# Splitting the weights of two products one product sooner and pinning activation splits behind them, in a retention and GLA layer

## The chip, the cores and the metric

The kernel runs on one core of a Trainium2 chip. The metric is device time in microseconds of one launch, the median of several runs. TensorE (PE) does the matmuls, VectorE (DVE) and ScalarE (ACT) the elementwise work, GpSimd (POOL) small vectors and adding DMAs, and SyncE (SP) issues most DMAs.

## The reference

One decoder layer over 512 rows and 16 meta rows of width 1024, in float32: an RMS norm, one wide input projection, a retention branch (4 heads, q and k of 256 with rope, v and gate of 512), a gated linear attention branch (4 heads), two branch projections, a merge by sigmoid gates, and an output projection with the residual and a last norm.

```python
u = rms_norm(h, norm_gain)
proj = u @ w_in
(rq, rk, rv, rg, gq, gk, gv, gg, glr, m_ret, m_gla) = jnp.split(proj, points, axis=-1)
rq = rope(rq.reshape(bsz, length, RET_HEADS, RET_QK_DIM), pos)
rk = rope(rk.reshape(bsz, length, RET_HEADS, RET_QK_DIM), pos) * (RET_QK_DIM ** -0.5)
o_ret = retention_chunked(rq, rk, rv)
o_ret = head_group_norm(o_ret, ...) * jax.nn.silu(rg)
...
merged = jax.nn.sigmoid(m_ret) * (o_ret @ w_branch_ret) + jax.nn.sigmoid(m_gla) * (o_gla @ w_branch_gla)
return h + merged @ w_out
```

## The kernel before

**Products in halves.** Every float32 operand of a matmul is split into a high half, which ACT casts (`nc.scalar.copy`), and a low half, which DVE takes as the difference; both are done by `split` (L163 in the profile). A product of two operands is then three matmuls: high by high, and the two mixed ones. For weights on the right side (`rows`) the order is high weight, low weight, high weight, so the second matmul of a product needs the low half.

**A quad.** Most projections go through `quad`, which computes a 1024 by 512 block with seven block products in place of eight (a Winograd form). In the order of the program these are products 1 (A11), 2 (A12), 6 (S2), 7 (S3), 5 (S1), 4 (A22) and 3 (S4). The name in brackets is the form of the activations, which is kept in both halves; the weights are split by `prepare`, which also keeps the pair of instructions in the list `low`. There are three buffers for each half, so a split has to wait until the product three before it is done. Three PSUM banks a, b and c take the sums: 1, 6, 5 and 3 go to b, 2 to a, 7 and 4 to c. Between the products `copy` brings a running sum out of PSUM (ACT), and `put` evacuates a finished quarter. Each product pins its first matmul behind the product before, so PE's order is the program's. Three flags move a split ahead of its product: `ahead` for product 2, `sooner` for product 6, `early` for another order of the products.

**Order of the work.** A planner orders the instructions of each engine: among those that it holds to be ready, the one that the program emitted first goes first. `after(a, b)` adds an edge that only tells the planner to put a behind b on their engine. `weave(dense, chain)` emits one step of the dense work (a product) and then one of the chain (smaller work).

**Heads 0 and 3.** For these two, the gate projection `ret_g` and the value projection `ret_v`, fourteen products, are the dense work. The chain is `ret_rope` (rope of k, split of k, rope of q, split of q: six steps) and then `ret_scores`. `every` adds, after each two steps of the rope, one step of the attention of the head before (`at`; none in head 0). In `ret_g` product 2's split is ahead. Its outputs carry the names rg_, those of `ret_v` rv_. The split q (qh, ql) is what the first score product needs, which stands on PE behind product 6 of `ret_v`. In `ret_v` the sums of raw weights stand at L364 and L365 (x3, x1), L381 (w11, which becomes product 6's) and L388 (w21, product 4's). Heads 1 and 2 order this work otherwise.

**Output projection.** Columns 0 to 255 are done plainly, columns 256 to 767 by a quad (names wo_), and the last 256 plainly again. The quad's chain is `merged_sums`, which makes the forms of the merged activations: the S2 and S3 forms, S1, then S4 from sums at L1519. For a quarter with `put(0, 0)` DVE adds (L1601, L1604) and ACT takes squares (fsq, L1556) for the last norm.

Of the kernel before, what the change touches and what calls it, by code (L numbers as in the profile page):

```python
# [25 lines left out]
ALU = mybir.AluOpType  # L26
# [14 lines left out]
C_RQ, C_RK, C_RV, C_RG = 0, 1024, 2048, 4096  # L41
# [7 lines left out]
A11, A12, A22, S1, S2, S3, S4 = range(7)  # L49
# [60 lines left out]
def hybrid_kernel(ctx: ExitStack, tc: tile.TileContext, I, out: bass.AP):  # L110
    nc = tc.nc
# [50 lines left out]
    def split(hi, lo, src):  # L162
        return nc.scalar.copy(hi, src), nc.vector.tensor_sub(lo, src, hi.bitcast(F32))  # L163
# [3 lines left out]
    def after(ins, prev):  # L167

        tc.add_manual_dep(ins.ins, prev.ins.name, mybir.DependencyInfo(
            mybir.DependencyClass.NoSync, mybir.DependencyReason.DATA), reason="order on an engine")  # L170
# [42 lines left out]
    def weave(dense, chain, skip=0):  # L213

        for n, _ in enumerate(dense):
            tick()
            if n >= skip:
                next(chain, None)
        for _ in chain:
            pass  # L220

    def every(gen, n, m=1, other=None):

        for i, _ in enumerate(gen):
            yield
            if i % m == m - 1:
                for _ in range(n - m):
                    if other is not None:
                        next(other, None)
                    yield  # L230

    def run(*gens):
        for g in gens:
            yield from g
# [29 lines left out]
    low = []  # L264

    def quad(cols, rows, name, evac, meta=None, adds=True, ahead=False, behind=None, src=None,
# [33 lines left out]
        if wide:  # L300
            a, b = [[ppt(f"{name}_{x}{t}")[:, :HT] for t in range(2)] for x in "cb"]
            c = a
# [13 lines left out]
        def product(i, form, w, ps, fresh, ready=None):  # L316
            hi, lo = ready or prepare(i, w)
            n = HT if wide and i not in (3, 5) else 256
            for t in range(2):
                col = slice(t * P, (t + 1) * P)  # L320
                for kk in range(4):
                    u = [row(f[form], kk)[:, col] if rows else row(f[form], kk)[:, :n] for f in forms]
                    v = [f[:, kk, :] if rows else f[:, kk, col] for f in (hi, lo)]
                    first = fresh and kk == 0 and (wide or t == 0)
                    for j, (x1, x2) in enumerate(((0, 0), (0, 1), (1, 0))):
                        l, r = (u[x1], v[x2]) if rows else (v[x1], u[x2])
                        m = nc.tensor.matmul(ps[t][:, :n] if wide else ps[t], l, r, start=first and j == 0,  # L327
                                             stop=kk == 3 and j == 2,
                                             skip_group_check=not fresh or not wide and t == 1)
                        if t == kk == j == 0:  # L330
                            pin(m)
            order[:] = [m]
# [13 lines left out]
        def put(n, th, x, y):  # L346
            evac(n, th, x if wide else x[2], y)
# [31 lines left out]
        else:  # L379
# [13 lines left out]
                late.append(lambda: meta(psm))  # L393
            yield
        product(5, S1, x1, b, False, ready)
        put(1, 1, b, x7)
        run_late()
        yield
        product(4, A22, w21, c, False)
        ready = prepare(3, w22) if early else None  # L400
        put(0, 1, c, y)
        yield
# [831 lines left out]
    def rope(t, c, name, prev=None):  # L1234

        def view(m):
            return m[:, :t.shape[2] * t.shape[3]].rearrange("p (h c) -> p h c", h=2)

        m = [view(rp.tile([P, 2 * HT], F32, tag="tmp", name=f"{name}_{i}", bufs=7)) for i in range(4)]
        x = nc.vector.tensor_mul(m[0], t[:, 0], c[0])  # L1240
        if prev is not None:
            after(x, prev)
            after(nc.vector.tensor_mul(m[1], t[:, 1], c[1]), prev)
        else:
            nc.vector.tensor_mul(m[1], t[:, 1], c[1])
        nc.vector.tensor_sub(m[0], m[0], m[1])
        yield
        nc.vector.tensor_mul(m[2], t[:, 1], c[0])
        nc.vector.tensor_mul(m[3], t[:, 0], c[1])
        nc.vector.tensor_add(m[2], m[2], m[3])  # L1250
        yield
        R[name] = m[0], m[2]
# [15 lines left out]
    def ret_rope(h):  # L1268
        q, k = R["raw", h]
        yield from rope(k, (cs[:, 0], cs[:, 1]), f"rpk{h}", None if h % 3 else low[1])  # L1270
        kh = rp.tile([P, 2, 2, HT], F32R, tag="kh", name=f"kh{h}")
        kl = rp.tile([P, 2, 2, HT], F32R, tag="kl", name=f"kl{h}")
        for i, m in enumerate(R[f"rpk{h}"]):
            split(kh[:, i], kl[:, i], m)
        for r in range(4):
            nc.gpsimd.tensor_copy(km[:, :, 32 * r:32 * r + NM].rearrange("p k (h m) -> p k h m", h=2),
                                  (kh if r < 3 else kl)[:, :, :, 256:HT].bitcast(F32))
        yield
        yield from rope(q, (cs[:, 0, :, :256], cs[:, 1, :, :256]), f"rpq{h}")
        qh = rp.tile([P, 2, T], F32R, tag="qh", name=f"qh{h}")  # L1280
        ql = rp.tile([P, 2, T], F32R, tag="ql", name=f"ql{h}")
        R["qk", h] = qh, ql, kh, kl
        for i, m in enumerate(R[f"rpq{h}"]):
            split(qh[:, i].rearrange("p (h c) -> p h c", h=2), ql[:, i].rearrange("p (h c) -> p h c", h=2), m)
        yield

    def ret_g(h):
        sg = rp.tile([P, 2304], F32, tag="sg", name=f"sg{h}")[:, :2048].rearrange("p (b c) -> p b c", b=NTB)
        R["sg", h] = sg
        yield from quad((C_RG + h * 512, C_RG + h * 512 + 256), True, f"rg{h}", rows_into(sg, AF.Silu),  # L1290
                        ahead=h % 3 == 0, behind=R.get(("pow", h - 1)))

    def ret_v(h):
        vh = rp.tile([P, NTB, 512], F32R, tag="vh", name=f"vh{h}")
        vl = rp.tile([P, 2176], F32R, tag="vl", name=f"vl{h}")[:, :2048].rearrange("p (b c) -> p b c", b=NTB)
        R["v", h] = vh, vl

        def meta(psm):
            ps = meta_rows(psm, f"rvm{h}")
            vm = rp.tile([P, 512], F32R, tag="vm", name=f"vm{h}")  # L1300
            nc.scalar.copy(vm, ps)
            nc.vector.tensor_sub(vm[64:96], ps[64:96], vm[64:96].bitcast(F32))
            R["vm", h] = vm

        def evac(n, th, x, y):
            if y is not None:
                s = tmp2(f"vs{h}{n}{th}")
                total(s, x, y)
                x = s
            d = slice(2 * th, 2 * th + 2), slice(n * 256, (n + 1) * 256)  # L1310
            hi, lo = vh[:, d[0], d[1]], vl[:, d[0], d[1]]
            if n == 0:
                split(hi, lo, x)
            else:
                nc.scalar.mul(hi, x, -1.0)
                nc.vector.scalar_tensor_tensor(lo, x, -1.0, hi.bitcast(F32), op0=ALU.mult, op1=ALU.subtract)

        yield from quad((C_RV + h * 512, C_RV + h * 512 + 256), True, f"rv{h}", evac, meta, False)

    def ret_scores(h):  # L1320
        qh, ql, kh, kl = R["qk", h]
# [152 lines left out]
    for h in range(4):  # L1474
        if h == 0:
            drain(ret_qk(h))
        else:
            at = ret_attention(h - 1)
            weave(ret_qk(h), at if h < 3 else islice(at, NTB + 1))
        if h % 3:  # L1480
            g = gates_gla(h - 1)
            weave(run(islice(g, 2), turns(ret_branch(h - 1), g)), ret_rope(h), skip=2)
            weave(ret_g(h), ret_scores(h))
            drain(ret_v(h))
        else:
            weave(run(ret_g(h), ret_v(h)), run(every(ret_rope(h), 3, 2, at if h else None), ret_scores(h)))
    weave(gates_ret(), ret_attention(3))

    def rows4(t, o, w, c):
# [9 lines left out]
    def merged_sums():  # L1499

        a = [[sigr[2 * kh + j][:, :, th * 256:(th + 1) * 256] for j in range(2)] for th in range(2) for kh in range(2)]
        a00, a01, a10, a11 = a

        def parts_of(i, x):
            for j in range(2):
                split(mforms[0][i][:, 2 * j:2 * j + 2], mforms[1][i][:, 2 * j:2 * j + 2], x[j])

        for j in range(2):
            nc.vector.tensor_sub(a11[j], a11[j], a10[j])
            nc.vector.tensor_sub(a10[j], a00[j], a10[j])  # L1510
        for j in range(2):
            nc.vector.scalar_tensor_tensor(a00[j], a11[j], -1.0, a00[j], op0=ALU.mult, op1=ALU.subtract)
        parts_of(S2, a00)
        yield
        parts_of(S3, a10)
        yield
        parts_of(S1, a11)
        for j in range(2):
            nc.vector.scalar_tensor_tensor(a01[j], a00[j], -1.0, a01[j], op0=ALU.mult, op1=ALU.subtract)  # L1519
        yield  # L1520
        parts_of(S4, a01)
        yield


# [124 lines left out]
```

## Time and profile before

| | |
|---|---|
| median of 3 runs | 751.62 us (750.5 to 751.65) |
| the profiled execution | 750.33 us |
| its span, first to last instruction | 748.6 us |
| ACT busy | 450.3 us (60%) |
| HBM read, written | 104.44 MB, 11.53 MB |

A row of a timeline gives the start in us, the duration in us, engine, line, operation, names (written, then read), shapes and, in brackets, idle time of the engine before it and what ended it. A row ending in x2 stands for two instructions in one. In a row of the list of waits stand the waiting instruction, what it waited for, the total in us, how often, and the longest. A matmul's end is modelled, its start is recorded.

### The profile page before, as it was taken

To read this page: it belongs to the slowest core of one execution; us is meant where nothing else is said; L and a number is where in the kernel's file an instruction comes from. 1 tells how busy PE (TensorE), PEld (TensorE's weight loads), DVE (VectorE), ACT (ScalarE), POOL (GpSimd) and SP (SyncE) were. 2 spreads that over 40 slices of the span, in tenths; PEclk is the share of its full clock that TensorE was granted. 3 is DMA by queue.
4 is the path that set the end of the run, shared out by engine and by line. 5 is a ranking of instruction groups with operands and counts; after the bars stand their busy time and mean duration, and the time that the engine had idled before them with its cause. 6 is when DMAs were issued, how large, how long until landed. Compare 5 with 4: busy or idle time off the path is not lost.

```text
span 748.6 us, 14064 instructions
## 1 busy us (share of the span) xinstructions
PE 738.6 (99%) x5595; PEld 691.7 (92%) x5595; DVE 607.7 (81%) x873; ACT 450.3 (60%) x764; POOL 137.5 (18%) x172
## 2 busy tenths in 40 slices
PE   9999999999999999999999999999999999999996
PEld 6799899989999999999989999989999989988996
DVE  6699877679897799888957688967697989775995
ACT  7898584666975466546546555646555656532562
POOL 2111110101221122110520100540011210111142
PEclk9999999999999999999999999999999999999999
DMA  9873521821589972734783652796476356687503
GB/s 298 278 162 77 121 62 53 198 85 58 129 187 280 305 169 87 170 113 141 200 250 115 133 149 96 199 213 163 126 169 136 113 141 197 227 195 206 133 29 113
DMA packets 100138, 117.42 MB, mean 157 GB/s; under 512 B 5732, under 2 KB 90852, under 8 KB 99816
## 3 DMA queue, kind: packets, MB, share of 16 engines
q1 hardware_dynamic: 79896, 88.19, 37.1%
q0 software_dynamic: 19888, 27.79, 20.4%
q8 instruction: 44, 0.72, 0.4%
q10 hardware_dynamic: 288, 0.53, 0.2%
q14 instruction: 22, 0.18, 0.1%
HBM read 104.44 MB, written 11.53 MB: 155 GB/s over the span
## 4 chain that ended last, share of the span: by engine, by line
PE 89%; DVE 7%; issue 2%; ACT 1%; POOL 0%; POOLq 0%; DVEq 0%; ACTq 0%
PE rqk_b L327 6%; PE rv_b L327 6%; PE rg_b L327 5%; PE rqk_c L327 5%; PE br_p L201 4%; PE br_p L202 4%; PE br_p L198 4%; PE gg_b L327 3%; PE mg_b L327 3%; PE mr_b L327 3%; PE gv_p L652 3%; PE rv_c L327 3%; PE bg_b L327 2%; PE rg_c L327 2%; PE gk_p L437 2%
## 5 line engine op out<-in xcount | busy, mean ns | idle before, releaser
L202 PE MATMUL br_p<-oh,br_l 128*128 128x512 f32 x128 | 49.9, 390 | 0.0
L201 PE MATMUL br_p<-ol,br_h 128*128 128x512 f32 x128 | 49.9, 390 | 0.0
L198 PE MATMUL br_p<-oh,br_h 128*128 128x512 f32 x128 | 49.8, 389 | 0.0
L163 ACT CAST rv_h<-rv_w 128x1024 fp32r<-128x1024 f32 x24 | 25.3, 1053 | 25.3 <-DVE rv_w L381 10.4
L327 PE MATMUL rqk_b<-xh,rqk_h 128*128 128x264 f32 (+1 forms) x128 | 36.2, 283 | 0.0
L327 PE MATMUL rqk_b<-xh,rqk_l 128*128 128x264 f32 (+1 forms) x128 | 36.1, 282 | 0.0
L327 PE MATMUL rqk_b<-xl,rqk_h 128*128 128x264 f32 (+1 forms) x128 | 36.0, 281 | 0.0
L327 PE MATMUL rv_b<-rv_l,xh 128*128 128x256 f32 x128 | 35.5, 277 | 0.5 <-DVE rv_l L163 0.5
L163 DVE TENSOR_TENSOR rv_l<-rv_w,rv_h 128x1024 fp32r<-128x1024 f32 x24 | 29.3, 1221 | 8.1 <-ACT rv_h L163 8.1
L327 PE MATMUL rv_b<-rv_h,xh 128*128 128x256 f32 x128 | 35.8, 280 | 0.0
L327 PE MATMUL rv_b<-rv_h,xl 128*128 128x256 f32 x128 | 35.4, 277 | 0.0
L327 PE MATMUL rg_b<-rg_h,xh 128*128 128x256 f32 x128 | 35.4, 277 | 0.0
L327 PE MATMUL rg_b<-rg_h,xl 128*128 128x256 f32 x128 | 35.4, 276 | 0.0
L327 PE MATMUL rg_b<-rg_l,xh 128*128 128x256 f32 x128 | 35.4, 276 | 0.0
L163 DVE TENSOR_TENSOR rg_l<-rg_w,rg_h 128x1024 fp32r<-128x1024 f32 x20 | 24.4, 1220 | 8.1 <-ACT rg_h L163 8.1
L163 ACT CAST rg_h<-rg_w 128x1024 fp32r<-128x1024 f32 x20 | 21.0, 1052 | 15.6 <-PE br_p L201 5.9
L291 POOL DMA_DIRECT2D rqk_x<-in_w_in_dram x8 | 10.4, 1302 | 102.2 <-PE rv_b L327 64.2
L202 PEld LDWEIGHTS br_p<-oh,br_l 128*128 128x128 f32 x128 | 24.0, 188 | 5.0
L1380 ACT ACTIVATE on<-av,nm,g_r 128x512 f32<-128x512 f32 x16 | 12.5, 779 | 26.4 <-DVE nm L1378 26.4
L198 PEld LDWEIGHTS br_p<-oh,br_h 128*128 128x128 f32 x128 | 24.0, 188 | 4.6
L201 PEld LDWEIGHTS br_p<-ol,br_h 128*128 128x128 f32 x128 | 24.0, 188 | 4.5
L163 ACT CAST rqk_h<-rqk_w 128x1024 fp32r<-128x1024 f32 x20 | 21.0, 1052 | 11.8 <-PE rqk_c L327 2.9
(624 smaller groups left out, 3155.4 us busy)
## 6 DMA issues: line engine op xcount, KB each, us to landing
rv_w<-in_w_in_dram SPq DMA_DIRECT2D x16, 512.0 KB, 4.2
br_w<-in_w_branch_ret_dram SPq DMA_DIRECT2D x16, 512.0 KB, 3.4
rqk_w<-in_w_in_dram SPq DMA_DIRECT2D x12, 512.0 KB, 5.0
rg_w<-in_w_in_dram SPq DMA_DIRECT2D x12, 512.0 KB, 4.9
rqk_x<-in_w_in_dram SPq DMA_DIRECT2D x8, 512.0 KB, 4.6
rqk_x<-in_w_in_dram POOLq DMA_DIRECT2D x8, 512.0 KB, 7.9
rg_x<-in_w_in_dram SPq DMA_DIRECT2D x8, 512.0 KB, 3.6
rg_x<-in_w_in_dram POOLq DMA_DIRECT2D x8, 512.0 KB, 7.6
```

Of the source, the lines that this page charges most:

```text
L163: return nc.scalar.copy(hi, src), nc.vector.tensor_sub(lo, src, hi.bitcast(F32))
L198: m = nc.tensor.matmul(o, lh, rh, start=first, stop=False)
L201: nc.tensor.matmul(o, lh, rl, start=False, stop=False)
L202: m = nc.tensor.matmul(o, ll, rh, start=False, stop=last)
L291: x = nc.gpsimd.dma_start(t, block(0, 1), accum_op=ALU.add)
L327: m = nc.tensor.matmul(ps[t][:, :n] if wide else ps[t], l, r, start=first and j == 0, stop=kk == 3 and j == 2, skip_group_check=not fresh ...
L437: m = nc.tensor.matmul(pss[t][th], l[:, kk, c], r, start=first and j == 0, stop=kh == 1 and kk == 3 and j == 2, skip_group_check=not meta ...
L652: m = nc.tensor.matmul(pss[t], (al if j == 1 else ah)[t // 2, kh][:, k, c], (lo if j == 2 else hi)[:, kk, :], start=q == kk == j == 0, sto ...
L1380: nc.scalar.activation(on, ps, AF.Identity, scale=r, bias=nm)
```

## The change

In `ret_g` of heads 0 and 3 the weights of product 4 are split before product 5's sum is evacuated. In `ret_v` of these heads the weights of product 6 are split before product 2's result is evacuated. In these heads the first two multiplications of q's rope are pinned behind the low half split last, and the splits of q come one step later and are pinned behind the pair split last. `every` now covers the first five steps of the rope, so the attention of the head before is stepped twice beside it. In the output projection the splits of S1, the sums for S4 and the splits of S4 come one or two steps later, and each is pinned behind the weights split last.

```diff
         product(5, S1, x1, b, False, ready)
+        ready = prepare(4, w21) if ahead else None
         put(1, 1, b, x7)
...
-        product(4, A22, w21, c, False)
+        product(4, A22, w21, c, False, ready)
...
-        yield from rope(q, (cs[:, 0, :, :256], cs[:, 1, :, :256]), f"rpq{h}")
+        yield from rope(q, (cs[:, 0, :, :256], cs[:, 1, :, :256]), f"rpq{h}", None if h % 3 else low[1])
...
+        if h % 3 == 0:
+            yield
+        prev = () if h % 3 else list(low)
         for i, m in enumerate(R[f"rpq{h}"]):
-            split(qh[:, i].rearrange("p (h c) -> p h c", h=2), ql[:, i].rearrange("p (h c) -> p h c", h=2), m)
+            s = split(qh[:, i].rearrange("p (h c) -> p h c", h=2), ql[:, i].rearrange("p (h c) -> p h c", h=2), m)
+            for ins, p in zip(s, prev):
+                after(ins, p)
...
-        yield from quad((C_RV + h * 512, C_RV + h * 512 + 256), True, f"rv{h}", evac, meta, False)
+        yield from quad((C_RV + h * 512, C_RV + h * 512 + 256), True, f"rv{h}", evac, meta, False, sooner=h % 3 == 0)
...
-            weave(run(ret_g(h), ret_v(h)), run(every(ret_rope(h), 3, 2, at if h else None), ret_scores(h)))
+            rp_h = ret_rope(h)
+            weave(run(ret_g(h), ret_v(h)), run(every(islice(rp_h, 5), 3, 2, at if h else None), rp_h, ret_scores(h)))
...
-        def parts_of(i, x):
+        def parts_of(i, x, prev=()):
             for j in range(2):
-                split(mforms[0][i][:, 2 * j:2 * j + 2], mforms[1][i][:, 2 * j:2 * j + 2], x[j])
+                s = split(mforms[0][i][:, 2 * j:2 * j + 2], mforms[1][i][:, 2 * j:2 * j + 2], x[j])
+                for ins, p in zip(s, prev):
+                    after(ins, p)
...
-        parts_of(S1, a11)
+        yield
+        parts_of(S1, a11, list(low))
+        yield
         for j in range(2):
-            nc.vector.scalar_tensor_tensor(a01[j], a00[j], -1.0, a01[j], op0=ALU.mult, op1=ALU.subtract)
-        yield
-        parts_of(S4, a01)
+            after(nc.vector.scalar_tensor_tensor(a01[j], a00[j], -1.0, a01[j], op0=ALU.mult, op1=ALU.subtract), low[1])
+        yield
+        parts_of(S4, a01, list(low))
         yield
```

## Prediction

> **What bounds the kernel now.** I read the page first, for which engine sets the time; then the list of PE's waits, for where PE stands; then PE's timeline at those places, since a matmul's end is modelled and only starts can be trusted; last the timelines of DVE and ACT there, for what is late.
>
> ```profile
> span 748.6 us, 14064 instructions
> PE 738.6 (99%) x5595; PEld 691.7 (92%) x5595; DVE 607.7 (81%) x873; ACT 450.3 (60%) x764; POOL 137.5 (18%) x172
> ```
>
> PE is nearly always at work, so a change that leaves PE's instructions alone (this one adds and removes no matmul) can only win the time in which PE stands.
>
> ```profile
> PE rg_c L327 <- DVE rg_l L163: 0.6, 1, 0.6
> PE wo_c L327 <- DVE wo_l L163: 0.5, 1, 0.5
> PE rv_b L327 <- DVE rv_l L163: 0.5, 1, 0.5
> PE wo_b L327 <- ACT wo_x L343: 0.3, 1, 0.3
> ```
>
> Each of these waits occurs once in the whole run. The first and third lie in head 3 and the other two in the output projection, as the next view shows; head 0, which runs the same code as head 3, has none.
>
> ```profile
> 593.22 0.28 PE L327 MATMUL rg_c<-rg_h,xh 128*128 128x256 f32 x1
> 594.11 0.39 PE L327 MATMUL rg_c<-rg_l,xh 128*128 128x256 f32 x1 [0.62 <-DVE rg_l L163]
> 594.34 0.28 PE L327 MATMUL rg_c<-rg_h,xl 128*128 128x256 f32 x1
> ...
> 607.14 0.28 PE L327 MATMUL rv_b<-rv_h,xh 128*128 128x256 f32 x1
> 607.93 0.38 PE L327 MATMUL rv_b<-rv_l,xh 128*128 128x256 f32 x1 [0.51 <-DVE rv_l L163]
> ...
> 718.95 0.28 PE L327 MATMUL wo_c<-wo_h,msh 128*128 128x256 f32 x1
> 719.75 0.39 PE L327 MATMUL wo_c<-wo_l,msh 128*128 128x256 f32 x1 [0.52 <-DVE wo_l L163]
> ...
> 722.26 0.28 PE L327 MATMUL wo_c<-wo_l,msh 128*128 128x256 f32 x1
> 722.37 0.28 PE L327 MATMUL wo_c<-wo_h,msl 128*128 128x256 f32 x1
> 722.96 0.39 PE L327 MATMUL wo_b<-wo_h,mh 128*128 128x256 f32 x1 [0.31 <-ACT wo_x L343]
> 723.29 0.39 PE L327 MATMUL wo_b<-wo_l,mh 128*128 128x256 f32 x1
> 723.51 0.28 PE L327 MATMUL wo_b<-wo_h,ml 128*128 128x256 f32 x1
> ```
>
> The undisturbed pace is 0.11 us from start to start (722.26 to 722.37). Start to start minus the pace is what a wait costs, which is more than the list of waits says. Product 4 of ret_g in head 3: 0.89 - 0.11 = 0.78, and the next matmul comes 0.23 - 0.11 = 0.12 late as well: 0.90. I take the same 0.12 behind the next two waits too, as an estimate. Product 6 of ret_v: 0.79 - 0.11 + 0.12 = 0.80. Product 7 of the output projection: 0.80 - 0.11 + 0.12 = 0.81. Product 5 there: 0.59 - 0.11 = 0.48 for the first matmul, 0.33 - 0.11 = 0.22 for the second (the weight's low half), 0.22 - 0.11 = 0.11 for the third: 0.81. All four together are 3.3 us. That is the most that the four places can give.
>
> **Head 3.** In each of them the second matmul is late, the one that needs the low half of the split weights, which DVE makes.
>
> ```profile
> 587.91 1.05 ACT L163 CAST rg_h<-rg_w 128x1024 fp32r<-128x1024 f32 x1
> ...
> 588.13 1.22 DVE L163 TENSOR_TENSOR rg_l<-rg_x,rg_h 128x1024 fp32r<-128x1024 f32 x1
> 589.26 0.68 DVE L844 TENSOR_TENSOR sg<-rg_a,rg_x 128x512 f32<-128x512 f32 x1
> ...
> 592.84 1.22 DVE L163 TENSOR_TENSOR rg_l<-rg_w,rg_h 128x1024 fp32r<-128x1024 f32 x1
> ...
> 595.51 0.68 DVE L844 TENSOR_TENSOR sg<-rg_b,rg_x 128x512 f32<-128x512 f32 x1
> ```
>
> *Product 4 split a product sooner, q's rope behind it.* The high half was ready at 588.96 (587.91 + 1.05); the low half ran only at 592.84. Between lie evacuations and, emitted before product 4, q's first rope step. With the split emitted before both and q's two first multiplications pinned behind it, the low half can run from 589.26 and end by 590.5, against PE's 593.33. That holds even if an evacuation or two of 0.6 go first. So this wait goes: 0.90. What is late next is DVE itself. Product 3 adds into the same PSUM bank that the evacuation at 595.51 reads until 596.19, and PE, 0.90 earlier, would come at about 596.0 (product 4's first matmul at 593.22, and 24 at 0.11 to 0.12). So some 0.2 us of a new wait is likely there. It does not enter the sum, because the next point decides.
>
> ```profile
> 599.64 0.68 DVE L163 TENSOR_TENSOR ql<-rpq,qh 128x512 fp32r<-128x512 f32 x1
> 600.25 1.22 DVE L364 TENSOR_TENSOR rv_x<-rv_w,rv_w 128x1024 f32<-128x1024 f32 x1
> 601.38 0.68 DVE L163 TENSOR_TENSOR ql<-rpq,qh 128x512 fp32r<-128x512 f32 x1
> ...
> 604.25 1.22 DVE L381 TENSOR_TENSOR rv_w<-rv_w,rv_x 128x1024 f32<-128x1024 f32 x1
> 605.50 1.23 DVE L388 TENSOR_TENSOR rv_w<-rv_w,rv_w 128x1024 f32<-128x1024 f32 x1
> 606.65 1.23 DVE L163 TENSOR_TENSOR rv_l<-rv_w,rv_h 128x1024 fp32r<-128x1024 f32 x1
> ...
> 605.56 1.06 ACT L163 CAST rv_h<-rv_w 128x1024 fp32r<-128x1024 f32 x1 [0.30 <-DVE rv_w L381]
> ```
>
> *Product 6 split a product sooner, q's splits behind it.* Not one of DVE's rows here has idle time in front: DVE is the bound of this stretch, and what lies ahead of product 6's low half (606.65) decides. Emitting the split sooner gains nothing by itself. The sum L381 ends at 605.47, ACT casts from 605.56 to 606.62, and L388 just fills DVE's hole meanwhile. What gains is that q's two differences leave the queue ahead: 0.61 (599.64 to 600.25) and, at the same size, 0.6. The low half then starts at 605.45, and the second matmul, now at 607.93, comes at 606.73. PE, freed of the first wait, would ask for it at 607.14 - 0.90 + 0.11 = 606.35, or up to 0.2 later if the evacuation above holds it. DVE stays the later one, so head 3 gives 607.93 - 606.73 = **1.2 us**, not 1.70. Bounds: 1.70 if DVE has less ahead of it than I count, 0 if other work takes the place of q's. Below nothing only if q's halves now come too late for the scores; that is a rival below. Behind the pinned splits are queued product 7's split and the value evacuations. PE leaves product 6 for the first score product and needs q's halves there:
>
> ```profile
> 610.66 0.40 PE L198 MATMUL sc<-qh,kh 128*128 128x512 f32 x1
> ...
> 299.65 0.40 PE L198 MATMUL sc<-qh,kh 128*128 128x512 f32 x1
> ...
> 295.34 1.22 DVE L163 TENSOR_TENSOR rv_l<-rv_w,rv_h 128x1024 fp32r<-128x1024 f32 x1
> ```
>
> At 610.66 - 1.2 = 609.5 in head 3. The low half ends at about 606.6, one evacuation (0.6) and the two q differences (1.2) end at 608.4: 1.1 to spare. In head 0 the low half now ends at 296.56 and will end no later, q's at 298.4 at most, against 299.65. So **head 0: 0**; it has no wait to lose, and keeps 1.2 us of cover.
>
> No step that is moved issues a DMA, and SP's and POOL's queues keep their order. The attention of the head before is stepped twice instead of three times beside the rope, but by then it has one half-turn left to emit, so nothing moves. Heads 1 and 2 take no new edge.
>
> **Output projection.**
>
> ```profile
> 714.20 1.05 ACT L163 CAST wo_h<-wo_x 128x1024 fp32r<-128x1024 f32 x1
> ...
> 715.52 1.83 DVE L163 TENSOR_TENSOR ml<-sigr,mh 128x512 fp32r<-128x512 f32 x2
> 717.28 1.28 DVE L1519 SCALAR_TENSOR_TENSOR sigr<-sigr,sigr 128x512 f32<-128x512 f32 x2
> 718.48 1.21 DVE L163 TENSOR_TENSOR wo_l<-wo_x,wo_h 128x1024 fp32r<-128x1024 f32 x1
> 720.82 0.68 DVE L1604 TENSOR_TENSOR hs<-hs,wo_x 128x512 f32<-128x512 f32 x1
> ...
> 721.53 0.42 ACT L1556 ACTIVATE fsq<-hs 128x256 f32<-128x256 f32 x1 [1.37 <-DVE hs L1604]
> 722.35 0.56 ACT L343 COPY wo_x<-wo_b 128x512 f32<-128x512 f32 x1
> ```
>
> *S1 behind product 7's weights.* Product 7's high half is ready at 715.25, but S1's two differences and S4's two sums stand ahead on DVE until 718.48. Pinned behind, they free the place at 715.52: the low half ends at 716.7, PE asks at 719.06, and 0.81 goes with 2.3 us of cover. *The copy of product 6's sum.* PE's second wait is for the copy at 722.35, which on ACT follows the squares at 721.53, which wait for the sum L1604 at 720.82, late behind the same S1 and S4 work. The L1519 pair (1.2) and S4's split leave its way. At worst S1's two differences stay ahead of it: the low half ends at 716.7, then 1.2 for these, 0.6 for the sum before L1604 and 0.6 for itself, which makes 719.1. The squares take 0.82 (721.53 to 722.35) and end near 720.0, the copy (0.56) near 720.6; PE would ask at 722.48 - 0.81 = 721.7. The 0.81 goes too, with 1.1 of cover. *S4 behind products 5 and 4.* Its sums and splits are 4 x 0.6 = 2.4 us of DVE work, moved and not added. They are needed by product 3, two products of 24 matmuls (2.7 each) after product 5's start; DVE then has three weight differences (1.15 each, the step from 605.50 to 606.65) beside them, so it is through in time. **1.6 us**, bounds 0.8 (the copy stays late) and 1.6.
>
> **Sum.** 1.2 + 0 + 1.6 = 2.8 us. The work in between is paced by PE, so the gain is carried to the end. The profiled execution took 750.33 us (748.6 of span) and would be 747.5. The median shown is 751.62, with runs from 750.5 to 751.65, and 751.62 - 2.8 = 748.8 is the forecast.
>
> **Rivals.** *A: DVE keeps head 3.* If the low half of product 6 is queued straight behind L381, L388 no longer fills the hole in which ACT casts (1.15, from 605.50 to 606.65), and product 7's split and q's halves come that much later; head 3's 1.2 is lost there again. Against it: the planner filled that hole before. Time: 751.62 - 1.6 = 750.0. [...]
>
> *B: given back.* New waits of the size of those removed, at the evacuation of 595.51 and around S4, take 2.8 back: 751.6. For it: two of my covers are 1.1 us. Against it: the only place where I find PE ahead of what it needs is product 3 of ret_g, and there by 0.2.
>
> *C: slower, by q's halves.* The pin takes whatever pair was split last when q's splits are emitted. If that pair belonged to a later product (4), whose buffer comes free only as product 6 ends, PE would stand at the first score product for a cast (1.06), a difference (1.15) and q's two (1.2): 3.4 us in each of heads 0 and 3, so 751.62 - 2.8 + 6.8 = 755.6. It decides from a lateness of 2.8 + 1.5 = 4.3 over both heads. Against it: the product's step is emitted before q's in the same turn, so the pair is product 6's. *D: it does not do what it says*, since edges change only the planned order and the planner already orders so: true of head 0, contradicted by the rows for the rest; it is within B.
>
> **How the numbers follow.** Forecast 0.64, A 0.20, B 0.10, C 0.06. The low end is 747.5, the profiled execution's time less 2.8. The high end leaves out B and C (0.16): it is A with the copy still late, 0.8, less 0.3 of a new wait: 751.1. A measurement of this kernel can tell about 0.2%, 1.5 us, from no change. The forecast lies beyond that, A on the line: faster 0.64 x 0.97 + 0.2 x 0.45 = 0.71, slower 0.06, same 0.23.
>
> **What would show it.** Right: PE's list of waits without wo_c and wo_b, rg_c without its 0.6, rv_b at most 0.4; DVE's ql behind product 6's rv_l in heads 0 and 3; wo_l for product 7 straight behind product 6's; a span of 745.8. Wrong: a new PE wait at sc (C), at rg_b for ACT or DVE at product 3, or DVE idle before product 6's rv_l (A); or waits in heads 1 and 2, which I hold untouched.

## The result and the profile after

The changed kernel takes **748.37 us** (median of 18 runs, 747.8 to 750.52) against 750.97 us (18 runs, 749.88 to 752.43) for the kernel before on the same chip. The ratio is 0.9969, 95% interval 0.9961 to 0.9977: 750.97 x 0.0031 = 2.3 us faster, 1.7 to 2.9 (the two medians alone lie 2.6 apart). The forecast was 748.8, from 2.8 us.

The profiled execution of the kernel after took 750.22 us, hardly less than the 750.33 of before. Here is the head of its page, and then two rows of its list of PE's waits (the waiting instruction, what it waited for, total, how often, longest).

```profile
span 748.4 us, 14064 instructions
PE 739.1 (99%) x5595; PEld 692.2 (92%) x5595; DVE 608.5 (81%) x873; ACT 449.7 (60%) x764; POOL 135.7 (18%) x172
```

```profile
PE bg_b L327 <- DVE gs L1153: 0.9, 1, 0.9
...
PE rg_b L327 <- DVE sg L845: 0.2, 1, 0.2
```

The engines do the same work as before (DVE 608.5 against 607.7): it was moved, not removed. All four waits that the prediction listed (rg_c, rv_b, wo_c, wo_b) are gone from the list. Two are new: rg_b, 0.2, which the prediction expected at product 3 of ret_g, and bg_b, 0.9, at a place that the change does not touch. The next view, PE's timeline of the kernel after, shows this one.

```profile
228.89 0.38 PE L327 MATMUL bg_b<-gs,bg_h 128*128 128x256 f32 x1
230.15 0.39 PE L327 MATMUL bg_b<-gs,bg_h 128*128 128x256 f32 x1 [0.88 <-DVE gs L1153]
```

This is in the GLA branch, ahead of head 0: 1.26 us from one matmul to the next. With 0.8 us that PE was late ahead of it, this hides the gain in this execution's span, so the span alone says nothing of the change. What can be read is PE's order, which is the same in both kernels: 5595 matmuls, one for one. I took the start of the same matmul in both traces and looked at how the difference changes from one landmark to the next. The landmarks are, in the kernel before: 239.97 (past the GLA wait), 299.65 (head 0's first score product), 591.97 (in head 3's ret_g, ahead of product 4), 610.66 (head 3's first score product) and 742.26 (the last matmul). Negative is earlier. All runs below are in the same table; each is told in its place. (The 0.19 of sums_both in head 0 is no single gap: it builds up in steps of under 0.02.)

| kernel | to 239.97 | head 0 | between | head 3 | output | all behind 239.97 |
|---|---|---|---|---|---|---|
| after | 2.12 | 0.00 | 0.02 | -1.05 | -1.21 | -2.23 |
| after_again (the same kernel) | 0.23 | 0.00 | 0.08 | -1.09 | -1.23 | -2.23 |
| heads_only | -0.03 | 0.00 | 0.06 | -1.11 | -0.03 | -1.07 |
| out_only | 3.99 | 0.00 | 0.03 | 0.02 | -1.20 | -1.15 |
| gate_only | 0.48 | 0.50 | 0.06 | 0.01 | -0.01 | 0.56 |
| value_nopin | 0.49 | 0.48 | 0.06 | -0.03 | -1.20 | -0.69 |
| s1_only | 0.63 | 0.00 | 0.01 | -1.07 | -0.82 | -1.88 |
| s4_only | 0.78 | 0.00 | 0.03 | -1.04 | -1.13 | -2.14 |
| sums_head | 0.55 | 0.00 | 0.02 | -1.70 | -1.27 | -2.95 |
| sums_both | 0.81 | 0.19 | 0.03 | -1.68 | -1.66 | -3.13 |
| sums_both_again | 1.42 | 0.00 | 0.08 | -1.67 | -1.69 | -3.27 |
| pool_out (leaves work out) | 0.80 | 0.00 | 0.02 | -1.04 | -1.67 | -2.69 |

The change gives 2.23 us in the trace: head 3 gives 1.05, the output projection 1.21, head 0 nothing. That agrees with the 2.3 of the times. PE's timeline of the kernel after at the four places and at the two new gaps:

```profile
595.37 0.28 PE L327 MATMUL rg_c<-rg_h,xh 128*128 128x256 f32 x1
595.48 0.28 PE L327 MATMUL rg_c<-rg_l,xh 128*128 128x256 f32 x1
...
597.97 0.28 PE L327 MATMUL rg_c<-rg_h,xl 128*128 128x256 f32 x1
598.48 0.36 PE L327 MATMUL rg_b<-rg_h,xh 128*128 128x256 f32 x1 [0.23 <-DVE sg L845]
598.68 0.28 PE L327 MATMUL rg_b<-rg_l,xh 128*128 128x256 f32 x1
...
608.85 0.28 PE L327 MATMUL rv_b<-rv_h,xh 128*128 128x256 f32 x1
608.99 0.39 PE L327 MATMUL rv_b<-rv_l,xh 128*128 128x256 f32 x1
609.22 0.28 PE L327 MATMUL rv_b<-rv_h,xl 128*128 128x256 f32 x1
...
720.04 0.28 PE L327 MATMUL wo_c<-wo_h,msh 128*128 128x256 f32 x1
720.16 0.28 PE L327 MATMUL wo_c<-wo_l,msh 128*128 128x256 f32 x1
...
722.65 0.28 PE L327 MATMUL wo_c<-wo_h,msl 128*128 128x256 f32 x1
722.76 0.28 PE L327 MATMUL wo_b<-wo_h,mh 128*128 128x256 f32 x1
...
728.09 0.28 PE L327 MATMUL wo_c<-wo_h,ml 128*128 128x256 f32 x1
728.48 0.36 PE L327 MATMUL wo_b<-wo_h,msh 128*128 128x256 f32 x1
728.68 0.28 PE L327 MATMUL wo_b<-wo_l,msh 128*128 128x256 f32 x1
```

Product 4 of ret_g runs at the pace of 0.11 (595.37 to 595.48), and so do products 7 and 5 of the output projection. Product 6 of ret_v is all but there: 0.14 and 0.23 instead of 0.11, 0.15 in all. Two gaps opened. At product 3 of ret_g PE goes from 597.97 to 598.48 and on to 598.68: 0.51 - 0.11 and 0.20 - 0.11, or 0.49. At product 3 of the output projection it goes from 728.09 to 728.48 and 728.68: 0.28 + 0.09 = 0.37. This second gap is not in the list of waits: the modelled end of the matmul before (728.09 + 0.28 = 728.37) leaves only 0.11 us of idle time, and the list shows nothing under 0.2.

DVE's timeline of the kernel after in head 3 (PE is 2.14 us later here than before, so 2.14 comes off when a time is set beside the prediction's):

```profile
592.40 1.22 DVE L163 TENSOR_TENSOR rg_l<-rg_w,rg_h 128x1024 fp32r<-128x1024 f32 x1
...
595.92 0.68 DVE L1247 TENSOR_TENSOR rpq<-rpq,rpq 128x512 f32<-128x512 f32 x1
596.52 1.22 DVE L163 TENSOR_TENSOR rg_l<-rg_w,rg_h 128x1024 fp32r<-128x1024 f32 x1
597.65 0.68 DVE L845 TENSOR_TENSOR sg<-rg_b,rg_x 128x512 f32<-128x512 f32 x1
...
604.06 1.22 DVE L365 TENSOR_TENSOR rv_w<-rv_w,rv_w 128x1024 f32<-128x1024 f32 x1
605.31 1.23 DVE L381 TENSOR_TENSOR rv_w<-rv_w,rv_x 128x1024 f32<-128x1024 f32 x1
606.57 1.22 DVE L388 TENSOR_TENSOR rv_w<-rv_w,rv_w 128x1024 f32<-128x1024 f32 x1
607.72 1.22 DVE L163 TENSOR_TENSOR rv_l<-rv_w,rv_h 128x1024 fp32r<-128x1024 f32 x1
608.86 1.29 DVE L163 TENSOR_TENSOR ql<-rpq,qh 128x512 fp32r<-128x512 f32 x2
```

Product 4's low half (592.40) now ends 1.75 us before PE starts the product. Product 6's low half (607.72) has q's differences behind it. Product 3 of ret_g waits for the evacuation L845 (597.65 to 598.33), in front of which stand a difference of q's rope (595.92) and product 3's own split (596.52).

The same for the output projection, DVE, then POOL (2.14 - 1.05 = 1.09 later than before, until product 7):

```profile
716.65 1.77 DVE L163 TENSOR_TENSOR wo_l<-wo_x,wo_h 128x1024 fp32r<-128x1024 f32 x1
...
720.14 0.68 DVE L1615 TENSOR_TENSOR hs<-hs,wo_x 128x512 f32<-128x512 f32 x1
...
721.88 1.28 DVE L1530 SCALAR_TENSOR_TENSOR sigr<-sigr,sigr 128x512 f32<-128x512 f32 x2
723.22 1.62 DVE L163 TENSOR_TENSOR wo_l<-wo_w,wo_h 128x1024 fp32r<-128x1024 f32 x1
...
725.97 1.76 DVE L163 TENSOR_TENSOR wo_l<-wo_w,wo_h 128x1024 fp32r<-128x1024 f32 x1
727.66 0.68 DVE L1612 TENSOR_TENSOR wo_x<-wo_b,wo_x 128x512 f32<-128x512 f32 x1
```

```profile
715.72 1.62 POOL L1571 TENSOR_TENSOR hs<-hs,fgb 128x256 f32<-128x256 f32 x1
...
722.57 1.19 POOL L1571 TENSOR_TENSOR hs<-hs,fgb 128x256 f32<-128x256 f32 x1
...
725.46 1.19 POOL L1571 TENSOR_TENSOR hs<-hs,fgb 128x256 f32<-128x256 f32 x1
```

Product 7's low half (716.65) stands 3.4 us ahead of its product. Product 3 waits for the evacuation of 727.66, which ends at 728.34. In front of it lie S4's sums and splits, and the low halves of products 4 and 3, which took 1.62 and 1.76 us where this difference takes 1.22 in head 3. Both lie beside a POOL multiplication.

### The profile page after: what moved, and what is told of

Same layout as the page of the kernel before. It is cut to its first block, busy times and chain, and to the rows that moved or that the text cites. A ratio compares the mean times of both kernels' runs of the same rounds, so it can differ in the third digit from the quotient of the medians.

```text
span 748.4 us, 14064 instructions
## 1 busy us (share of the span) xinstructions
PE 739.1 (99%) x5595; PEld 692.2 (92%) x5595; DVE 608.5 (81%) x873; ACT 449.7 (60%) x764; POOL 135.7 (18%) x172
## 4 chain that ended last, share of the span: by engine, by line
PE 90%; DVE 3%; ACT 2%; DMA 2%; issue 1%; POOL 1%; POOLq 0%; DVEq 0%; ACTq 0%
PE rqk_b L327 6%; PE rv_b L327 6%; PE rg_b L327 5%; PE rqk_c L327 5%; PE br_p L201 4%; PE br_p L202 4%; PE br_p L198 4%; PE gg_b L327 3%; PE gv_p L653 3%; PE mg_b L327 3%; PE rv_c L327 3%; PE rg_c L327 2%; PE mr_b L327 2%; PE bg_b L327 2%; PE gg_c L327 2%; PE gk_p L438 2%
```

## The experiments

The theory after the result: the gain has two independent parts, each worth what its waits held less what the next DVE item takes back. The rival: one part gives all of it and the other is neutral, or the GLA stage answers to the change. Each diff is against the kernel after the change.

In the heads' diffs the call of `every` goes back with the rope and is left out here.

**Each half alone.** heads_only puts the output projection's order back:

```diff
-        yield
-        parts_of(S1, a11, list(low))
-        yield
+        parts_of(S1, a11)
         for j in range(2):
-            after(nc.vector.scalar_tensor_tensor(...), low[1])
+            nc.vector.scalar_tensor_tensor(...)
         yield
-        parts_of(S4, a01, list(low))
+        parts_of(S4, a01)
```

> The changes in heads 0 and 3 alone; the output projection as before. Theory (DVE is the bound of head 3, and only what leaves its queue ahead of product 6's low half counts): 1.05 us less than before, 749.9, with the wait of product 4 gone, about 0.5 of new wait at product 3 for the evacuation, and some 0.1 left at product 6 of the value projection; head 0 without any wait. Rival (each removed PE wait is worth its own length): 1.7 less, 749.3. Rival (all the gain is in the output projection): 751.0.

749.87 us against 751.38, ratio 0.9989 (0.9979 to 0.9998). In the trace head 3 gives 1.11 and the output projection 0.03.

out_only puts the heads back:

```diff
-        ready = prepare(4, w21) if ahead else None
+        ready = None
...
-        yield from rope(q, ..., f"rpq{h}", None if h % 3 else low[1])
+        yield from rope(q, ..., f"rpq{h}")
...
-        if h % 3 == 0:
-            yield
-        prev = () if h % 3 else list(low)
+        prev = ()
...
-        yield from quad(..., meta, False, sooner=h % 3 == 0)
+        yield from quad(..., meta, False)
```

> The change in the output projection alone; heads 0 and 3 as before. Theory (two waits of 0.8 go, one new of 0.36 comes at product 3): 1.25 us less than before, 749.7, and with the heads alone it adds up to the whole change (1.05 + 1.25 = 2.3). Rival (the two places are not independent, since the earlier stage sets when weights land): less than 0.8 or more than 1.6.

749.68 us, ratio 0.9982 (0.9973 to 0.9991): 1.35 us. In the trace the output projection gives 1.20 and head 3 nothing. The two halves make 1.07 + 1.15 = 2.22 of the whole's 2.23, so they are independent.

**What in head 3 gives the gain.** gate_only keeps only product 4's sooner split and the pin of q's rope behind it; q's later splits with their pins, `sooner` in ret_v and the whole output part are undone.

```diff
-        if h % 3 == 0:
-            yield
-        prev = () if h % 3 else list(low)
+        prev = ()
...
-        yield from quad(..., meta, False, sooner=h % 3 == 0)
+        yield from quad(..., meta, False)
```

> Only product 4's split a product sooner and q's first rope step behind it, in heads 0 and 3; the value projection, q's splits and the output projection as before. Theory (DVE has no idle time between this place and product 6's low half in the value projection): the 0.90 wait goes, about 0.5 comes back at product 3, the rest is added to the wait at product 6, and the time is that of before, 751.0 within 0.3. Rival (the wait is worth its length): 0.4 to 0.9 less, 750.1 to 750.6.

751.29 us, ratio 1.0002 (0.9994 to 1.0011). The wait at product 4 is gone, and head 3 still gives nothing. PE's timeline of gate_only at product 6 of ret_v, in head 0 and in head 3:

```profile
297.91 0.38 PE L327 MATMUL rv_b<-rv_l,xh 128*128 128x256 f32 x1 [0.21 <-DVE rv_l L163]
...
608.95 0.38 PE L327 MATMUL rv_b<-rv_l,xh 128*128 128x256 f32 x1 [0.53 <-DVE rv_l L163]
```

and ahead of it, at product 2 of ret_v in head 3:

```profile
605.00 0.28 PE L327 MATMUL rv_a<-rv_h,xh 128*128 128x256 f32 x1
605.41 0.38 PE L327 MATMUL rv_a<-rv_l,xh 128*128 128x256 f32 x1
```

Head 0, which had no wait at product 6, now loses 0.50 there. In head 3 the wait at product 6 is what it was, 0.53 against 0.51, and not longer as expected. The 0.90 is lost before it: 0.45 at product 3 of ret_g, and 0.41 at product 2 of ret_v, whose second matmul comes 0.41 behind the first and whose third 0.22 behind the second (0.30 + 0.11 over the pace). Product 2's low half ends at 605.36 here, which is 604.32 on the clock of before (1.04 us of lag), and ended at 604.34 there. So the 0.90 of product 4 is not a gain by itself: DVE is the bound of the stretch, and pushing q's rope back leaves the low halves behind it where they were, or, in head 0, later.

value_nopin is the whole change except q's later splits and their pins.

```diff
-        if h % 3 == 0:
-            yield
-        prev = () if h % 3 else list(low)
+        prev = ()
```

> The whole change except that q's splits are neither pinned nor a step later. Theory (splitting product 6 sooner gains nothing by itself; the two differences of q that leave DVE's queue are the gain of head 3): q's two differences stand ahead of product 6's low half again, PE's wait there is about 1.2 where the whole change has 0.1, and the time is 1.05 above the whole change, 749.4. Rival (the sooner split is what counts): as the whole change, 748.4.

750.33 us, ratio 0.9992 (0.9982 to 1.0001): slower than the expectation. The output projection gives its 1.20, head 3 only 0.03, and head 0 loses 0.48, which I had not counted. The wait at product 6 of head 3 was expected to grow to about 1.2; it stays as before (0.82 from start to start against 0.79), and 0.41 is lost at product 2 as in gate_only. DVE's timeline of value_nopin at product 6:

```profile
602.39 0.69 DVE L163 TENSOR_TENSOR ql<-rpq,qh 128x512 fp32r<-128x512 f32 x1
...
606.52 1.23 DVE L388 TENSOR_TENSOR rv_w<-rv_w,rv_w 128x1024 f32<-128x1024 f32 x1
607.66 1.22 DVE L163 TENSOR_TENSOR rv_l<-rv_w,rv_h 128x1024 fp32r<-128x1024 f32 x1
```

q's differences are back ahead of the low half, and L388 is still ahead of it, although its split is emitted sooner. The sooner split of product 6 does nothing without the pins: heads 0 and 3 are as in gate_only. Putting q's splits later and pinning them is what turns head 3's 0.03 into 1.05, and it keeps head 0 at zero. The pins without the two sooner splits were not run, so what these splits add to them is not shown.

**What in the output projection gives the gain.** s1_only keeps S1's pin; S4's sums and splits go back to their places without pins.

```diff
         parts_of(S1, a11, list(low))
-        yield
         for j in range(2):
-            after(nc.vector.scalar_tensor_tensor(...), low[1])
+            nc.vector.scalar_tensor_tensor(...)
         yield
-        parts_of(S4, a01, list(low))
+        parts_of(S4, a01)
```

> The whole change, but in the output projection only S1's splits are moved and pinned; the sums for S4 and its splits carry no pin. Theory (what stands on DVE ahead of product 7's low half and ahead of the first quarter's sum decides): the S4 sums (1.2) stand ahead of product 7's low half in S1's place, so that wait still goes (0.8); the first quarter's sum comes only 0.6 earlier than before the change, so some 0.2 to 0.4 of the wait for the copy is left. 748.4 to 748.9. Rival (S1's pin does nothing, S4's everything): 749.7.

748.23 us against 751.06, ratio 0.9964 (0.9951 to 0.9976). The times cannot tell it from the whole; the trace can: 0.82 instead of 1.21. Nothing is gained at product 5 (0.01), so the wait for the copy cost its whole 0.8, which the expectation had wrong. From the list of waits and DVE's timeline of s1_only:

```profile
PE wo_b L327 <- ACT wo_x L343: 0.6, 1, 0.6
```

```profile
715.12 1.83 DVE L1529 SCALAR_TENSOR_TENSOR sigr<-sigr,sigr 128x512 f32<-128x512 f32 x2
716.87 1.21 DVE L163 TENSOR_TENSOR wo_l<-wo_x,wo_h 128x1024 fp32r<-128x1024 f32 x1
```

Without a pin S4's sums slip ahead of product 7's low half, and take 1.83 there, not the 1.28 of the kernel after. The sum before the squares, and so the copy, stands behind them: it starts at 719.81, 720.24 on the clock of before (0.43 us of lead), where the kernel after has 720.14 - 1.09 = 719.05.

s4_only keeps S4's pins; S1's splits go back.

```diff
         parts_of(S3, a10)
         yield
+        parts_of(S1, a11)
         yield
-        parts_of(S1, a11, list(low))
         yield
```

> The whole change, but in the output projection only the sums for S4 and its splits are moved and pinned; S1's splits stay where they were. Theory: S1's two differences (1.2, up to 1.8 beside POOL) stand ahead of product 7's low half, which still ends before PE asks for it; no wait at product 7, none for the copy, the same 0.36 at product 3 as in the whole change; 748.4, so S1's pin adds nothing that S4's does not give. Rival (both pins are needed, half of the 1.25 each): 749.0.

748.8 us, ratio 0.9967 (0.9956 to 0.9979); the trace has 1.13 of the 1.21. S4's pins do nearly all; S1's, which alone give 0.82, add about 0.1 to them.

**What the two new gaps cost.** sums_head takes two of q's DVE operations out of the way in heads 0 and 3: the difference of the first rope step is pinned behind the evacuation L845, and the sum of the second step is emitted only after product 6's low half. No operation is added.

```diff
-            nc.vector.tensor_add(dst, p, q)
+            R["sum"] = nc.vector.tensor_add(dst, p, q)
...
-        nc.vector.tensor_sub(m[0], m[0], m[1])
+        x = nc.vector.tensor_sub(m[0], m[0], m[1])
+        if late:
+            after(x, R["sum"])
...
-        nc.vector.tensor_add(m[2], m[2], m[3])
+        if not late:
+            nc.vector.tensor_add(m[2], m[2], m[3])
...
+            if i and h % 3 == 0:
+                after(nc.vector.tensor_add(m, m, R[f"rpq{h}"][2]), low[1])
```

> The whole change, and in heads 0 and 3 the difference that ends q's first rope step also waits for the evacuation that product 3 of the gate projection waits for, and the sum that ends q's second rope step goes behind product 6's split. Theory (DVE's queue up to product 6's low half sets head 3): 0.6 leaves that queue, the 0.48 at product 3 goes and the 0.1 at product 6 does not come back; 0.55 less than the whole change, 747.8. Rival (the order inside the stretch is without effect, since DVE works without a pause): 748.4.

748.05 us, ratio 0.9961 (0.9947 to 0.9975). Head 3 gives 1.70 in the trace, the prediction's upper bound, and the list of PE's waits has no rg_b. In DVE's timeline of sums_head the evacuation now has the difference L1247 behind it:

```profile
595.47 0.68 DVE L845 TENSOR_TENSOR sg<-rg_b,rg_x 128x512 f32<-128x512 f32 x1
596.07 0.68 DVE L1247 TENSOR_TENSOR rpq<-rpq,rpq 128x512 f32<-128x512 f32 x1
```

sums_both adds the same for the output projection: product 3's weights are split a step sooner, with the low half pinned behind the evacuation L1612.

```diff
+        if hold:
+            ready = prepare(3, w22)
+            after(low[1], R[hold])
         product(3, S4, w22, b, False, ready)
...
-            nc.vector.tensor_add(q, p, q)
+            R["wo", n, th] = nc.vector.tensor_add(q, p, q)
...
-    weave(quad((256, 512), True, "wo1", evac_wo, src=I["w_out"], forms=mforms), merged_sums())
+    weave(quad((256, 512), True, "wo1", evac_wo, src=I["w_out"], forms=mforms, hold=("wo", 1, 1)), merged_sums())
```

> As sums_head, and in the output projection product 3's low half goes behind the evacuation of product 5's sum, for which product 3's first matmul waits. Theory: the 0.36 at product 3 goes as well; 0.9 less than the whole change, 747.4, and the fastest of all so far. Rival (the low half is then late in its place): 747.8 as sums_head or above.

748.01 us, ratio 0.9964 (0.9951 to 0.9977): by the times no better than sums_head. The trace has 1.68 and 1.66, with no wait left in either stretch. To tell it, it ran once more, with the kernel after on the same chip.

> The whole change once more, beside the next kernel on one chip. Theory: as measured, 0.3% below the kernel before, with the new waits at product 3 of the gate projection (0.48) and of the output projection (0.36).

> The version with the two evacuations first, once more, beside the whole change on one chip. Theory: its trace has none of the two waits at product 3 and none at product 6, 0.9 less than the whole change. Rival: the 0.9 is lost elsewhere and the two are alike within 0.2.

Before 750.63, after_again 748.81 (ratio 0.9971, 0.996 to 0.9983), sums_both_again 747.62 (0.9952, 0.9933 to 0.9971). The trace has 2.23 against 3.27. So a version that beats both kernels exists, by about 1.1 us over the change; since the two intervals overlap, that rests on the traces more than on the times. The trace of after_again has no bg_b in its list of waits, and its span is 746.5: the 0.9 in the GLA stage belongs to the execution, not to the kernel.

**Is POOL the cause of the second gap?** pool_out leaves two of POOL's multiplications out.

```diff
-        if o < 512:
+        if o < 512 and not (o == 256 and t < 2):
             nc.gpsimd.tensor_mul(hh, hh, fgb[:, o:o + 256])
```

> The whole change, but two of POOL's multiplications by the norm's gain (rows 0 to 255, columns 256 to 511) are left out of the output projection. Theory (POOL's multiplication and DVE's differences take turns at the same memory, so a weight difference of 1.22 takes 1.62 to 1.77 while it runs): the differences of products 4 and 3 take 1.22 again and the wait of 0.36 at product 3 is gone or under 0.1. Rival (the long rows are some other stall, and the wait at product 3 comes from the order alone): the differences stay at 1.6 and more, the wait at 0.3.

One run of 748.54 us, which says nothing by itself. DVE's timeline of pool_out:

```profile
715.33 1.77 DVE L163 TENSOR_TENSOR wo_l<-wo_x,wo_h 128x1024 fp32r<-128x1024 f32 x1
...
721.90 1.23 DVE L163 TENSOR_TENSOR wo_l<-wo_w,wo_h 128x1024 fp32r<-128x1024 f32 x1
...
724.37 1.23 DVE L163 TENSOR_TENSOR wo_l<-wo_w,wo_h 128x1024 fp32r<-128x1024 f32 x1
```

The two differences are back at 1.23, product 7's, whose POOL neighbour stayed, is still 1.77, and the output projection gives 1.67 instead of 1.21. So without POOL's two multiplications the gap is not there. The order has its part too: sums_both keeps them, with one difference at 1.63, and closes the gap (1.66) by letting the evacuation go ahead of product 3's low half.

## Why the prediction was right, point by point

- **PE is the bound, and only its standing time can be won.** Right: the order of PE did not change, and the gain is the waits removed less the gaps opened. The upper limit of 3.3 us for the four places was nearly reached by sums_both (3.13 and 3.27). Of the other signs named for right, q's differences behind product 6's low half and product 7's low half straight behind product 6's were seen, and heads 1 and 2 did not move (0.02).
- **Product 4 of ret_g loses its 0.90.** Right. PE's lag behind before falls from 2.14 (595.37 - 593.22, both rounded) to 1.19 over this product, a gain of 0.95.
- **"Some 0.2 us of a new wait" at product 3.** Right place, too small: 0.49. I took the evacuation at its old place and only moved PE ahead. But the evacuation was itself pushed back: it started at 595.51 before and at 597.65 - 2.14 = 595.51 now, behind a rope difference and product 3's split. It stayed exactly where it was while PE came 0.95 sooner. The prediction lists a wait at rg_b both as likely and as a sign of being wrong, so this sign came; it is part of what B below took back.
- **DVE bounds product 6, and head 3 gives 1.2.** The mechanism was right: gate_only and value_nopin show that the sooner splits gain nothing in head 3 without q's pins, although there the bound shows at product 2 already, which the prediction did not look at. The size was 1.05 to 1.11. The low half was to start at 605.45 and started at 607.72 - 2.14 = 605.58. The 0.13 is in the steps between differences: 604.06 to 605.31 is 1.25, while the next item starts 1.13 behind such a difference elsewhere (596.52 to 597.65). L381 overwrites what L365 reads, and with product 2's split out of between, the two now stand next to each other. Counting 0.6 for each removed item misses what such an item hides. That this is the cause of the 0.13 is my estimate from these rows; no run tested it.
- **Head 0: 0.** Right. In the trace of the kernel after, head 0's product 6 low half ends at 296.16 and q's halves at 297.37 on the clock of before (2.12 us of lag), against the score product at 299.65: the cover was 2.3, more than the 1.2. What could be lost was ahead of that, at product 6 itself: in gate_only its low half starts 0.8 later than before (296.63 - 0.48 against 295.34), and 0.5 is lost.
- **Product 7 and the copy: 1.6.** Right up to product 5. PE's start against before went from 720.04 - 718.95 = 1.09 late to 0.52 early (the third matmul of product 5), which is 1.61. The sum before the squares was to end at 719.1 at the latest; L1615 ended at 720.82 - 1.09 = 719.7, 0.6 later, because product 7's low half took 1.77 and not 1.2. The copy had cover enough.
- **S4 "is through in time".** Wrong, and the term that failed: product 3 waits 0.37, and 0.1 more of the lead goes by the end, which I did not trace to a cause (pool_out and sums_both, which close the gap, do not lose it). I priced the weight differences beside S4 at 1.15 each, from an undisturbed row in head 3. The trace of before had 1.73 for just this one, and I used a row from another stage. From 721.88 to the evacuation at 727.66 DVE took 5.78. With 1.22 for the two slowed differences it would have been 0.40 + 0.54 = 0.94 less, and the evacuation would have ended at 727.4, ahead of PE's 728.2. pool_out shows it.
- **The sum:** 1.2 + 0 + 1.6 = 2.8 became 1.05 + 0 + 1.21, 2.23 by the trace and 2.3 by the times. The forecast of 748.8 was still near 748.37, because it started from 751.62, the median of three runs, where 18 runs have 750.97. The base was 0.65 too high and the gain 0.5 too large; the two errors offset each other, so that the time came so near is luck.
- **The span of 745.8** was not seen, 748.4 instead, because of 2.12 us ahead of 239.97. after_again had 746.5 with 0.23 there.
- **Rival A** (DVE keeps head 3): not so. L388 (606.57) still fills the hole ahead of the low half (607.72). A's condition, the low half queued straight behind L381, did not come about, so what it would have cost was not shown. **B** (given back): it said all 2.8, and that did not happen; it is true for 0.65 of head 3's 1.70 and 0.45 of the output projection's 1.66. **C** (q's halves late): they end at 610.15 against the first score product at 611.76. What a pin behind a later pair would cost was not tried. **D:** not so.

## What to carry to other kernels

When one engine is the bound of a stretch, removing a single wait ahead of it can gain nothing (gate_only: 0.01 us from head 3, with the 0.90 of product 4 gone): look for what can leave the queue altogether until the last deadline, here q's splits and S4's sums, and check the twin stage (head 0) whose cover the same move eats. When a consumer comes sooner, ask of each buffer that it refills whether the evacuation in front of it comes sooner as well. Take a duration from the same operation in the same stage, beside the same neighbours, not from a quiet one: the weight difference of 1.22 took 1.62 and 1.76 beside POOL.

## What the hardware showed that I had not expected

**POOL and DVE hold each other up.** The rows of the kernel after, shown above: the DVE differences from 716.65, 723.22 and 725.97 overlap POOL's multiplications by 0.69, 0.54 and 0.68 us and take 0.55, 0.40 and 0.54 more than 1.22: each time the overlap less 0.14. POOL's multiplications take 1.19 to 1.62, where an undisturbed one took 0.73 in the kernel before (L1560 there; DVE stands from 732.58 to 734.41):

```profile
733.03 0.73 POOL L1560 TENSOR_TENSOR hs<-hs,fgb 128x256 f32<-128x256 f32 x1
```

In these rows the two take turns, to within 0.14: each of the three differences ends 1.08 after POOL's multiplication, and each of the three multiplications 0.60 or 0.61 after the DVE row that ran as it began (ends at 716.73, 723.16 and 726.05). Not every pair does so: L1617, 0.68 from 732.58, runs beside a multiplication of 0.74 from 732.76 in the kernel after, and neither is longer than alone (0.69 at 728.37, and the 0.73 above). What the two engines share, a memory as the theory of pool_out has it or something else, no run shows.

**The GLA stage differs from execution to execution.** PE's landmark at 239.97 came -0.03 to 3.99 us against before, over twelve traces, and 2.12 and 0.23 in two of the same kernel. Not all of it belongs to this stage: in the kernel after, 0.45 was there at 10 us and 0.79 at 227. From there to 239.97 the traces lose 0.01 to 4.29 us against before, and 1.33 and 0.01 in the two of the same kernel. Where PE stands longest, in out_only, it waits for gs, and the chain that ended last leads from there back to an og DMA, which ended at 227.93:

```profile
217.30 10.63 DMA og<-og1gq
```

What makes this DMA late was not tested.

**The clock halved after a stand of under 3 us, in one execution.** In out_only PE started one matmul only, at 229.22, between 227.44 and 230.49: 2.8 us lost. The windows of out_only, with the number of PE's instructions in brackets after its busy time, and the granted clock third from the right:

```profile
230.00:231.00 1.00, 0.52 (x2) 0.52 (x3) 1.00 (x2) 1.00 (x2) 0.00 (x0) 0.62 1.08 353
231.00:232.00 1.00, 1.00 (x7) 1.00 (x6) 1.00 (x2) 0.06 (x1) 0.46 (x1) 0.50 0.77 265
...
233.00:234.00 1.00, 1.00 (x7) 1.00 (x7) 1.00 (x2) 0.00 (x0) 0.00 (x0) 0.67 1.02 271
234.00:235.00 1.00, 1.00 (x11) 1.00 (x10) 0.43 (x1) 0.16 (x1) 0.00 (x0) 1.00 0.88 96
```

For some 3 us PE starts 7 matmuls per us instead of 11. If the clock is either 1.00 or 0.50, the shares 0.62 and 0.67 put it at 0.50 from about 230.24, 2.8 us after the start at 227.44, to about 233.66: 3.4 us, an estimate from these windows. After the shorter stand in the kernel after (228.89 to 230.15) the clock stays at 1.00. What length of stand lowers the clock, and what brings it back, was not tested.
